# Second layer's first expert taken ahead of the overflow branch, its input by a one-hot product, and three more held weight tiles

## The chip, the cores and the metric

The kernel runs on one core of a Trainium2 chip. The metric is the device time of one execution in microseconds (us); lower is better. Weights lie in HBM and reach the core's SBUF by DMA in tiles of 512 KB. TensorE (PE) multiplies, VectorE (DVE) and ScalarE (ACT) do the elementwise work, GpSimd (POOL) issues the gathers and scatters, SyncE (SP) issues the weight loads in program order.

## What is computed

Two layers of a hybrid backbone over 256 latent and 256 context tokens of width 1024. Each layer has a token-mixing half and a mixture of 16 gated experts, of which every token uses two. The change lies in the experts of the second layer, where only the 256 latent tokens are left:

```python
def hier_moe(h, rg_w, rg_b, re_w, re_b, w_gate, w_up, w_down):
    tok = h.reshape(-1, shp[-1])
    glog = (tok @ rg_w + rg_b).astype(jnp.float32)
    gprob = jax.nn.softmax(glog, axis=-1)
    gsel = jnp.argmax(glog, axis=-1)
    ...
    top_v, top_i = lax.top_k(elog_sel, MOE_TOPK)
    top_w = jax.nn.softmax(top_v, axis=-1) * gp
    eidx = gsel[:, None] * MOE_PER_GROUP + top_i
    comb = jnp.sum(jax.nn.one_hot(eidx, N_EXPERTS, dtype=jnp.float32) * top_w[..., None], axis=1)
    out = jnp.zeros(tok.shape, jnp.float32)
    for e in range(N_EXPERTS):
        hid = jax.nn.silu(tok @ w_gate[e]) * (tok @ w_up[e])
        out = out + comb[:, e:e + 1] * (hid @ w_down[e])
```

The tokens of the change are those of `modulate(h_lat, ...)`, the normalized and modulated rows that go into `hier_moe`.

## The kernel before

**The stage.** `moe` (L1557) runs the 16 experts of a layer as places e = 0 to 15. Places 0 and 1 are the experts 0 and 1; the others are ordered by how many tokens they got, so their weights' addresses are read at run time from a table `permi`. In the second layer (`KINDS[1]`, L38) places 2, 4, 6 and 8 are heavy (up to 128 tokens, each weight split on ACT and DVE into a high and a low fp32r part, three products each) and the other twelve are light (up to 64 tokens, plain fp32 products). Each expert has 12 weight tiles of 512 KB: 4 gate, 4 up, 4 down.

**Routing, then a branch.** `route` (L1237) finds the experts of each token and the place of each token within its expert; `slots` (L1406) turns this into row indices by a product of a bf16 one-hot matrix with a small table; `light_g` (L1424) gathers the rows of an expert's tokens from a copy in HBM (`h2s`); `rank` (L1293) orders the experts and finds the largest overflow, `mxi`. Every engine reads `mxi` into a register (L1603) and jumps over a block for overflowing experts (L1604), which these inputs do not need. Only behind the branch come `by_rank` and `weights` on DVE, the transposes of the gathered rows (`light_x`, L1430) and the experts.

**The expert loop** (L1634). For each e: indices and gather of e + 2, transposes of e + 1, `hid(e)` (gate and up products, silu, product, transposes of the result), then `out(e - 1)` (down products, scaling, scatter to HBM). So the down tiles of an expert are used one expert later than its gate and up tiles: the order of use is gate and up of 0, gate and up of 1, down of 0, gate and up of 2, down of 1, and so on.

**The ring of weight tiles.** `wload2` (L1532) loads the next tile into the next place of a ring (`self.order`, L1574): 11 buffers of the rings `w` and `w2`, then tiles that are idle in this stage: 4 in `xl`, 4 in `merged`, and in the second layer 2 in `h`: 21 places. A load waits until the tile that was in its place has been used. 20 loads are issued ahead of the branch and kept in the list `hold` (L1593 to L1596): gate and up of 0 and 1, down of 0. The tile `xh` serves as four high and four low buffers for the splits (`whx`, `wlx`, L1568), beside rings of four `wh` and four `wl`. SP issues all loads in program order. All loads but those of places 0 and 1 stand behind the branch, each with its expert's number, which SP reads from `permi` (L1581).

All matmuls are recorded at L257, all transposes at L260, ACT's operations at L266 and DVE's products at L263 (helpers); tiles tell them apart.

Of the kernel before, what the change touches and what calls it, by code (L numbers as in the profile page):

```python
# [11 lines left out]
F32R = mybir.dt.float32r  # L12
# [3 lines left out]
ALU = mybir.AluOpType  # L16
AX = mybir.AxisListType
P = 128
# [170 lines left out]
class Build:  # L189
# [971 lines left out]
    def mix_out(self, l, ntt):  # L1161
        nc = self.nc
        nt = 128 * ntt
        ns = ntt // 2
        self.meta = self.sb([P, 4, 16, 9], "meta", BF16)
        stat = self.cb("meta").rearrange("p (t c) -> p t c", t=4)
        nc.gpsimd.tensor_copy(self.meta[:, :ntt], stat[:, :ntt, None, :].to_broadcast([P, ntt, 16, 9]))
        self.h = self.sb([P, 4, D], "h")
        for tt in range(ntt):
            self.load_h(l, tt, self.h[:, tt], nc.gpsimd)  # L1170
        mh = self.sb([P, KD, 512], "xh", F32R)
        ml = self.sb([P, KD, 512], "xl", F32R)
        for k in range(KD):
            self.act(mh[:, k, :nt], self.merged[:, k, :nt])
            self.tt(ml[:, k, :nt], self.merged[:, k, :nt], mh[:, k, :nt].bitcast(F32), ALU.subtract)
        s1 = self.sb([P, KD, 2], "ys1")
        s2 = self.sb([P, KD, 2], "ys2")
        m2 = self.modT[l][:, 2]
        nc.vector.tensor_scalar(s1, m2, 0.5, None, op0=ALU.mult)
        self.tt(s2, m2, self.pp("b_out")[:, :, None].to_broadcast([P, KD, 2]))  # L1180
        g1, b1 = self.row(l, "big", 0, 0), self.row(l, "big", 1, 0)
        ms = [(self.row(l, "mod", 3, s, "rowt2" if s else "rowt4"), self.row(l, "mod", 4, s, "rowt2" if s else "rowt4")) for s in range(ns)]
        yT = self.sb([P, KD, 512], "yT")

        def wout(s):
            c = slice(256 * s, 256 * s + 256)
            for dt in range(KD):
                hs = self.split(self.wload(self.a["wout"][l, dt]), pool=s == 0 and ns == 2)
                pt = self.ps()[:, :256]
                for k in range(KD):  # L1190
                    wh, wl = hs[k // 4]
                    q = slice(128 * (k % 4), 128 * (k % 4) + 128)
                    self.mm3(pt, wh[:, q], wl[:, q], mh[:, k, c], ml[:, k, c], k == 0, k == KD - 1)
                self.act(yT[:, dt, c], pt, AF.Identity, scale=s1[:, dt, s:s + 1], bias=s2[:, dt, s:s + 1])

        rw = self.rw.rearrange("p (k n) -> p k n", k=KD)
        plog = self.ps("g")
        def norms(tt):
            h1 = self.h[:, tt]
            x = self.sb([P, D], "xm")  # L1200
            for q in range(2):
                pt = self.ps()
                for k in range(4):
                    self.tr(pt[:, 128 * k:128 * k + 128], yT[:, 4 * q + k, 128 * tt:128 * tt + 128])
                c = slice(512 * q, 512 * q + 512)
                nc.vector.scalar_tensor_tensor(x[:, c], h1[:, c], ALPHA, pt, op0=ALU.mult, op1=ALU.add)
            self.norm_affine(h1, x, g1, b1, f"a{tt % 2}")
            m3, m4 = ms[tt // 2]
            self.norm_affine(x, h1, m4, m3, f"b{tt % 2}", x)
            nc.gpsimd.dma_start(self.h2s[128 * tt:128 * tt + 128, :], x)  # L1210
            return x

        def logits(tt, x):
            hT = self.sb([P, KD, P], "h2Tt")
            for q in range(2):
                pt = self.ps()
                for k in range(4):
                    self.tr(pt[:, 128 * k:128 * k + 128], x[:, 512 * q + 128 * k:512 * q + 128 * k + 128])
                self.act(hT[:, 4 * q:4 * q + 4, :].rearrange("p k t -> p (k t)"), pt)
            for k in range(KD):  # L1220
                self.mm(plog[:, 20 * tt:20 * tt + 20], hT[:, k, :], rw[:, k, :], k == 0, k == KD - 1)

        xs = {}
        for s in reversed(range(ns)):
            wout(s)
            for tt in (2 * s, 2 * s + 1):
                xs[tt] = norms(tt)
        for tt in range(2, ntt):
            logits(tt, xs[tt])
        self.pump(1)  # L1230
        logits(0, xs[0])
        logits(1, xs[1])
        self.pump(3)
        self.plog = plog
        self.dump(f"h1_{l}", self.h[:, :ntt])

    def route(self, l, ntt):  # L1237
# [48 lines left out]
        self.ix, self.m3 = self.sb([P, 16, 2], "ix", I32), self.sb([P, 16, 3], "m3")  # L1286
        stat = self.stat = self.cb("meta").rearrange("p (t c) -> p t c", t=4)
        self.slots([posm[:, :T, e] for e in range(2)], [stat] * 2, T, self.ix[:, 0:2], self.m3[:, 0:2], not KINDS[l][0])
        cnt = self.sb([P, 16], "cnt")
        v.scalar_tensor_tensor(cnt, pc[:, 64:80], 16.0, self.c("key0"), op0=ALU.mult, op1=ALU.add)  # L1290
        self.rt = gl, gmx, v1, v2, oh1, oh2, ohg, pc, cnt, posm1
# [132 lines left out]
    def light_g(self, ix, T):  # L1424
# [2 lines left out]
                                          in_offset=bass.IndirectOffsetOnAxis(ap=ix, axis=0), bounds_check=256 * T - 1, oob_is_err=False)  # L1427
        return xe

    def light_x(self, xe):  # L1430
        xT = self.sb([P, KD, P], "xTh")[:, 0:4]
        pt = self.ps("g")
        for k in range(4):
            self.tr(pt[:, 128 * k:128 * k + 128], xe[:, 128 * k:128 * k + 128])
        self.act(xT.rearrange("p k t -> p (k t)"), pt)
        return xT

    def light_hid(self, xT, wsrc):
        pgu = []
        for n in ("expert_w_gate", "expert_w_up"):  # L1440
            pt = self.ps()
# [12 lines left out]
        pt = self.ps("g")  # L1454
        for j in range(2):
            self.tr(pt[:, 128 * j:128 * j + 128], hid[:, 128 * j:128 * j + 128])
        hT = self.sb([P, 2, 512], "hidT")[:, 0, 0:256]
        self.nc.vector.tensor_copy(hT, pt[:, 0:256])
        return hT

# [69 lines left out]
                                          bounds_check=256 * T - 1, oob_is_err=False)  # L1530

    def wload2(self, src):  # L1532
        if self.hold:
            return self.hold.pop(0)
        r = self.order[self.wi % len(self.order)]
        t = self.sb([P, D], ("w", "w2")[r]) if r < 2 else self.wx[r - 2]
        self.wi += 1
        self.nc.sync.dma_start(t, src)
        return t

    def split2(self, w):
# [3 lines left out]
        for q in range(2):  # L1545
            self.si += 1
            j = self.si % self.sn
            if j < 4:
                hi, lo = self.whx[:, j], self.wlx[:, j]
            else:  # L1550
                hi, lo = self.sb([P, 512], "wh", F32R), self.sb([P, 512], "wl", F32R)
            self.act(hi, w[:, 512 * q:512 * q + 512])
            self.tt(lo, w[:, 512 * q:512 * q + 512], hi.bitcast(F32), ALU.subtract)
            hs.append((hi, lo))
        return hs

    def moe(self, l, ntt):  # L1557
        nc, tc = self.nc, self.tc
        T = ntt

        def wsrc(e, dyn):
            def f(n, u):
                if dyn:
                    return self.a[n][l, bass.ds(e, 1), u].rearrange("o p n -> (o p) n")
                return self.a[n][l, e, u]
            return f

        wx = self.sb([P, 8, 512], "xh", F32R)  # L1568
        self.whx, self.wlx = wx[:, 0:4], wx[:, 4:8]
        w3, w4 = self.sb([P, 4, D], "xl"), self.sb([P, 4, D], "merged")  # L1570
        self.wx = [w3[:, j] for j in range(4)] + [w4[:, j] for j in range(4)]
        self.wx += [self.h[:, j] for j in range(T, 4)]
        rings = (1, 0, 1, 1, 0, 1, 0, 1, 1, 0, 1) if KINDS[l][0] else (1, 0) * 5 + (1,)
        self.wi, self.order = 0, rings + tuple(range(2, 2 + len(self.wx)))  # L1574
        kind = KINDS[l]
# [11 lines left out]
        out = lambda e: (self.expert_out if kind[e] else self.light_out)(hd, wf(e), self.m3[:, e, 2:3], self.ix[:, e, 1:2], T)  # L1587
        slot = lambda e, p, m: self.slots([p[:, :T, SLOT_RANK[l][e]]], [m], T, self.ix[:, e:e + 1], self.m3[:, e:e + 1], not kind[e])
        self.route(l, T)
        g = [gather(0), gather(1)]  # L1590
        self.rank(l)
        self.pump(9)
        first = [wsrc(e, False)(n, u) for e in range(2) for n in ("expert_w_gate", "expert_w_up") for u in range(4)]  # L1593
        first += [wsrc(0, False)("expert_w_down", u) for u in range(4)]
        first = first[:len(self.order)]
        hold = [self.wload2(f) for f in first]  # L1596
        self.si = -1
        ready = [self.split2(hold[u]) for u in range(4)] if kind[0] else None
        st = self.wi, self.order
# [1 line left out]
        self.si, self.sn = -1, 4  # L1601
        tc.no_sync_barrier()
        most = nc.values_load(self.mxi[0:1, 0:1], min_val=0, max_val=576)  # L1603
        with tc.If(most > 128):  # L1604
            self.weights(T, self.by_rank(T))
            self.excess(l)
# [17 lines left out]
            self.si = -1  # L1624
            for u in range(2 if kind[0] else 0):
                self.split2(hold[u])
        self.si, self.sn = 2 * 4 - 1, 8
        self.ready = ready
        self.wi, self.order = st
        self.hold = hold  # L1630
        x, hd = getx(0), None
        oe = self.by_rank(T)
        for e in range(NE):
            if e + 2 < NE:  # L1634
# [9 lines left out]
            if e == NE - 1:  # L1644
                n = self.wi % len(self.order)
                self.wi, self.order = 0, tuple(r for r in self.order[n:] + self.order[:n] if r < 6)
            h2 = hid(e, x)
            if e:
                out(e - 1)
            if e == 0:  # L1650
# [54 lines left out]
    modT = {}  # L1705
    early = {}
    wi = si = 0
    hold = ready = None
    sn = 8

    def prologue(self, l):
# [60 lines left out]
```

## Time and profile before

| | us |
|---|---|
| median of 3 runs (lowest, highest) | 1880.85 (1872.6, 1885.78) |
| the profiled execution | 1872.98 |
| its span in the trace | 1871.2 |
| PE busy | 1716.1 (92%) |
| DVE busy | 1204.7 (64%) |
| ACT busy | 851.3 (45%) |
| POOL busy | 223.1 (12%) |

The 1.8 us between the execution's time and its span lie outside the trace. Times in rows are us from the span's start; the second layer's routing and experts take the stretch from about 1557 to 1845. A busy share is an average over many stages, so the part on the change reads one stage alone. fp32 products show as two rows per instruction.

### The profile page before, as it was taken

What the parts mean: (1) busy time and instruction counts of PE and PEld (TensorE: products, weight loads), DVE (VectorE), ACT (ScalarE), POOL (GpSimd) and SP (SyncE); (2) the same over time, 40 slices, a digit from 0 to 9 for tenths busy, and PEclk for the clock granted to TensorE, in tenths of its full rate; (3) what the DMA queues carried; (4) which work ended last, traced back from release to release, by engine and by line L of the source; (5) the groups of instructions that cost most, each with busy time, mean ns of one, the idle gap of its engine ahead of it and who ended that gap; (6) DMA issues with size and microseconds to landing.
All of it is one profiled execution on the core that took longest, in us unless ns stands there. A gap on an engine that the chain in (4) does not pass through costs nothing. (4 is left out here: it accounts for less than half of the span.)

```text
span 1871.2 us, 31716 instructions
## 1 busy us (share of the span) xinstructions
PE 1716.1 (92%) x11399; PEld 1268.0 (68%) x11399; DVE 1204.7 (64%) x2623; ACT 851.3 (45%) x1696; POOL 223.1 (12%) x321
## 2 busy tenths in 40 slices
PE   6999999998999999699999959999998995899984
PEld 1777777786777788377766516787898995566541
DVE  3878598287353547698575487698678766556203
ACT  3644553243233335187565536455555562455211
POOL 1011101000000205111111021100010100111210
PEclk9999999999999999899999979899999997899996
DMA  9221004523535745889999882231144584899993
GB/s 342 90 75 46 13 24 152 197 84 130 169 130 192 300 144 188 304 295 398 392 382 376 345 314 77 66 92 58 47 147 149 169 327 168 324 414 406 403 410 136
DMA packets 112732, 396.50 MB, mean 212 GB/s; under 512 B 16256, under 2 KB 16352, under 8 KB 112560
## 3 DMA queue, kind: packets, MB, share of 16 engines
q1 hardware_dynamic: 99120, 359.87, 52.6%
q0 software_dynamic: 13440, 34.44, 5.1%
q8 instruction: 94, 1.54, 0.3%
q14 instruction: 78, 0.64, 0.1%
HBM read 388.43 MB, written 17.35 MB: 217 GB/s over the span
## 5 line engine op out<-in xcount | busy, mean ns | idle before, releaser
L266 ACT ACTIVATE wh<-w 128x512 fp32r<-128x512 f32 x500 | 310.1, 630 | 416.8 <-PE psmm L257 293.0
L263 DVE TENSOR_TENSOR wl<-w,wh 128x512 fp32r<-128x512 f32 x484 | 333.3, 700 | 188.6 <-ACT wh L266 185.2
L257 PE MATMUL psmm<-xh,wh 128*128 128x256 f32 (+1 forms) x1280 | 440.1, 344 | 1.3 <-ACT wh L266 1.3
L257 PE MATMUL psmm<-xh,wl 128*128 128x256 f32 (+1 forms) x1280 | 434.8, 340 | 4.0 <-POOL wl L263 2.9
L257 PE MATMUL psmm<-xl,wh 128*128 128x256 f32 (+1 forms) x1280 | 433.1, 339 | 2.0 <-DVE xl L263 2.0
L257 PEld LDWEIGHTS psmm<-xh,wh 128*128 128x128 f32 x1280 | 243.1, 190 | 52.5 <-issue 16.0
L257 PEld LDWEIGHTS psmm<-xh,wl 128*128 128x128 f32 x1280 | 243.0, 190 | 38.7 <-issue 5.9
L257 PEld LDWEIGHTS psmm<-xl,wh 128*128 128x128 f32 x1280 | 243.3, 190 | 30.0 <-issue 3.9
L970 DVE SCALAR_TENSOR_TENSOR cx<-cbuf,part,cx 128x512 f32<-128x512 f32 (+1 forms) x240 | 143.0, 614 | 2.1
L257 PE MATMUL psmm<-br,wh 128*128 128x512 f32 (+1 forms) x512 | 127.9, 337 | 0.4 <-ACT cth L266 0.4
L263 DVE TENSOR_TENSOR hid<-hid,psmm 128x256 f32<-128x256 f32 (+1 forms) x32 | 17.2, 537 | 136.6 <-PE psmm L257 121.6
L257 PEld LDWEIGHTS psmm<-br,wh 128*128 128x128 f32 x512 | 87.6, 188 | 11.7 <-ACT cth L266 0.6
L263 DVE TENSOR_TENSOR xh<-w,xh 128x512 fp32r<-128x512 f32 x124 | 80.5, 686 | 18.9 <-ACT xh L266 17.9
L257 PE MATMUL psmm<-br,wl 128*128 128x512 f32 (+1 forms) x256 | 86.4, 338 | 1.1 <-DVE wl L263 1.1
L257 PE MATMUL psmm<-xh,xTh 128*128 128x512 f32 x224 | 79.4, 413 | 5.7 <-ACT xh L266 5.1
L266 ACT ACTIVATE xh<-w 128x512 fp32r<-128x512 f32 x124 | 72.2, 627 | 18.9 <-DMA w<-in_expert_w_gate_dram 7.2
L257 PE MATMUL psg<-w,silc 128*32 128x512 f32 x320 | 64.2, 651 | 16.3 <-DMA w<-in_wmod_dram 16.3
L257 PE MATMUL psmm<-w,xTh 128*64 128x256 f32 x560 | 67.6, 387 | 1.6 <-DMA w<-in_expert_w_up_dram 1.1
L266 ACT ACTIVATE ye<-psmm,m 128x512 f32<-128x512 f32 x46 | 30.3, 684 | 71.5 <-PE psmm L257 71.1
L257 PEld LDWEIGHTS psmm<-w,xTh 128*64 128x64 f32 x560 | 41.0, 139 | 26.6 <-issue 5.1
L257 PEld LDWEIGHTS psmm<-xh,xTh 128*128 128x128 f32 x224 | 40.9, 189 | 24.5 <-ACT xh L266 9.7
L266 ACT ACTIVATE xTh<-psg 128x512 fp32r<-128x512 f32 (+1 forms) x46 | 26.3, 598 | 65.4 <-PE psg L260 62.0
(471 smaller groups left out, 2847.0 us busy)
## 6 DMA issues: line engine op xcount, KB each, us to landing
w<-in_wch_dram SPq DMA_DIRECT2D x136, 512.0 KB
w<-in_wmod_dram SPq DMA_DIRECT2D x80, 512.0 KB
w<-in_expert_w_down_dram SPq DMA_DIRECT2D x77, 512.0 KB
w<-in_expert_w_gate_dram SPq DMA_DIRECT2D x76, 512.0 KB
w<-in_expert_w_up_dram SPq DMA_DIRECT2D x71, 512.0 KB
w<-in_wbr_dram SPq DMA_DIRECT2D x32, 512.0 KB
xl<-in_expert_w_up_dram SPq DMA_DIRECT2D x28, 512.0 KB
xl<-in_expert_w_gate_dram SPq DMA_DIRECT2D x26, 512.0 KB
```

What stands on the lines that cost most here:

```text
L257: self.nc.tensor.matmul(out, lhsT, rhs, start=start, stop=stop, **k)
L263: (eng or self.nc.vector).tensor_tensor(out, a, b, op)
L266: self.nc.scalar.activation(out, in_, func, **k)
L970: nc.vector.scalar_tensor_tensor(x, w, dw[:, c, k:k + 1], x, op0=ALU.mult, op1=ALU.add)
```

## The change

For a layer whose place 0 is light (the second one) the rows of expert 0 are no longer gathered from HBM. `light_x0` builds an fp32 one-hot matrix from the places found by `route` and multiplies it with the two token tiles that are still on chip (`self.h2t`), which gives the transposed input at once. `hid(0)` is emitted between the reading of `mxi` and the branch. The list `hold` becomes a table `held`, and loads are keyed by expert, name and tile. Three parts of `xh` join the ring of weight tiles (24 places), the fourth holds the input and the hidden rows of expert 0, and the splits of the second layer use the rings `wh` and `wl` alone. As many loads as the ring has places are issued ahead of the branch: the down tiles of expert 1 come to those of before.

```diff
+        self.h2t = xs
...
+        self.posm0 = posm[:, :T, 0]
...
+    def light_x0(self, T, xT):
+        oh = self.sb([P, 4, P], "oh")[:, :T, 0:64]
+        for tt in range(T):
+            self.nc.vector.tensor_scalar(oh[:, tt], self.cb("iota")[:, 0:64], self.posm0[:, tt:tt + 1], None, op0=ALU.is_equal)
+        pt = self.ps("g")
+        for k in range(KD):
+            o = 128 * (k % 4) + 64 * (k // 4)
+            for tt in range(T):
+                self.mm(pt[:, o:o + 64], self.h2t[tt][:, 128 * k:128 * k + 128], oh[:, tt], tt == 0, tt == T - 1, skip_group_check=True)
+        self.act(xT.rearrange("p k t -> p (k t)"), pt)
+        return xT
...
-        if self.hold:
-            return self.hold.pop(0)
+        if isinstance(src, tuple):
+            return src[0]
...
-            if j < 4:
+            if j < 4 and self.whx is not None:
...
-                return self.a[n][l, e, u]
+                return held.pop((e, n, u), self.a[n][l, e, u])
...
-        wx = self.sb([P, 8, 512], "xh", F32R)
-        self.whx, self.wlx = wx[:, 0:4], wx[:, 4:8]
+        if KINDS[l][0]:
+            wx = self.sb([P, 8, 512], "xh", F32R)
+            self.whx, self.wlx = wx[:, 0:4], wx[:, 4:8]
...
+        if not KINDS[l][0]:
+            self.whx = None
+            w5 = self.sb([P, 4, D], "xh")
+            self.wx += [w5[:, j] for j in range(3)]
...
-        g = [gather(0), gather(1)]
+        g = [gather(0), gather(1)] if kind[0] else [gather(1)]
+        x0 = None if kind[0] else self.light_x0(T, w5[:, 3, 0:512].rearrange("p (k t) -> p k t", k=4))
...
-        first = [wsrc(e, False)(n, u) for e in range(2) for n in ("expert_w_gate", "expert_w_up") for u in range(4)]
-        first += [wsrc(0, False)("expert_w_down", u) for u in range(4)]
-        first = first[:len(self.order)]
+        keys = [(e, n, u) for e in range(2) for n in ("expert_w_gate", "expert_w_up") for u in range(4)]
+        keys += [(e, "expert_w_down", u) for e in range(2) for u in range(4)]
+        keys = keys[:len(self.order)]
+        first = [wsrc(e, False)(n, u) for e, n, u in keys]
         hold = [self.wload2(f) for f in first]
+        held.update((k, (t,)) for k, t in zip(keys, hold))
...
         most = nc.values_load(self.mxi[0:1, 0:1], min_val=0, max_val=576)
+        h0 = None if kind[0] else self.light_hid(x0, wf(0), w5[:, 3, 512:768])
         with tc.If(most > 128):
...
-        x, hd = getx(0), None
+        x, hd = getx(0) if x0 is None else x0, None
...
-            h2 = hid(e, x)
+            h2 = h0 if e == 0 and h0 is not None else hid(e, x)
```

The order of instructions shows three places. First PE, second layer, from the jump over the overflow block on, in the kernel before (`xe_17765` and `xe_17769` are the gathered rows of experts 0 and 1, `oh_18569` the one-hot matrix for the indices of place 2, `w_...` weight tiles):

```order
L1604 UNCONDITIONAL_BRANCH x2
L260 MATMUL psg_18549<-ident_77,xe_17765 128x128 x4
L257 LDWEIGHTS oh_18569
L257 MATMUL psg_18568<-constb_79,oh_18569 128x9
L260 MATMUL psg_18581<-ident_77,xe_17769 128x128
L257 LDWEIGHTS oh_18569
L257 MATMUL psg_18568<-constb_79,oh_18569 128x9
L260 MATMUL psg_18581<-ident_77,xe_17769 128x128 x3
L257 MATMUL psmm_18587<-w_3365_17794,xTh_18548 64x256 x4
```

The transposes of expert 0, the indices of place 2 and the transposes of expert 1 stand ahead of the products of expert 0.

PE in the changed kernel, same stage, ahead of the branch (`xm_...` are the token tiles, `oh_17769` the new fp32 one-hot matrix, `xh_17702` the part that holds the input of expert 0):

```order
L257 MATMUL psg_17772<-oh_17769,xm_17590 128x64
L257 MATMUL psg_17772<-oh_17769,xm_17624 128x64
L257 MATMUL psmm_17861<-w_3366_17811,xh_17702 64x256 x4
L257 MATMUL psmm_17861<-w_17813,xh_17702 64x256 x4
L257 MATMUL psmm_17861<-w_3368_17815,xh_17702 64x256 x4
L257 MATMUL psmm_17861<-w_17817,xh_17702 64x256 x4
L257 MATMUL psmm_17878<-w_3370_17819,xh_17702 64x256 x4
L257 MATMUL psmm_17878<-w_17821,xh_17702 64x256 x4
L257 MATMUL psmm_17878<-w_3372_17823,xh_17702 64x256 x4
L257 MATMUL psmm_17878<-w_17825,xh_17702 64x256 x4
L260 MATMUL psg_17898<-ident_77,hid_17895 128x128 x2
L1626 TENSOR_LOAD mxi_17803
```

The pair of one-hot products stands there eight times; all of `hid(0)` on PE lies ahead of PE's reading of `mxi`, and on DVE and ACT their parts of it do too. Behind the branch PE now begins so:

```order
L1628 UNCONDITIONAL_BRANCH x2
L257 LDWEIGHTS oh_18768
L257 MATMUL psg_18767<-constb_79,oh_18768 128x9
L260 MATMUL psg_18780<-ident_77,xe_17765 128x128 x2
L257 LDWEIGHTS oh_18768
L257 MATMUL psg_18767<-constb_79,oh_18768 128x9
L260 MATMUL psg_18780<-ident_77,xe_17765 128x128 x2
L257 MATMUL psmm_18862<-w_3374_17827,xTh_18779 64x256 x4
```

The first thing there is the product for the indices of place 2, whose matrix DVE makes behind its own branch; the transposes of expert 1 (`xe_17765` here) and its gate products follow it.

On SP all 14 readings of `permi`, each with two register instructions, now stand between the reading of `mxi` and the branch; before, they stood behind it. The third place is SP behind the branch, at the 22nd to 25th load there in the kernel before (places 2 and 4; an ISA row sets the address register of a load):

```order
L1538 DMA h_17267<-in_expert_w_down_dram 128x1024
L1538 ISA
L1538 DMA w_3539_19048<-in_expert_w_down_dram 128x1024
L1538 ISA
L1538 DMA w_19064<-in_expert_w_down_dram 128x1024
L1538 ISA
L1538 DMA w_3556_19116<-in_expert_w_gate_dram 128x1024
```

The gate tiles of place 4 go into ring buffers `w` there, which had held gate and up tiles of place 2. In the changed kernel the same loads are the 19th to 22nd behind the branch:

```order
L1552 DMA merged_17701<-in_expert_w_down_dram 128x1024
L1552 ISA
L1552 DMA h_17267<-in_expert_w_down_dram 128x1024
L1552 ISA
L1552 DMA h_17267<-in_expert_w_gate_dram 128x1024
L1552 ISA
L1552 DMA xh_17702<-in_expert_w_gate_dram 128x1024
```

The four gate tiles of place 4 now go into the second part of `h` and the three parts of `xh`, where the down tiles of expert 1 are held.

## Rows read from the trace of the kernel before

**Rows 1.** Stretches of the stage: busy us of each engine (instructions), PE's granted clock, DMA share, GB/s

```profile
1550.00:1600.00 50.00, 24.43 (x153) 21.59 (x153) 32.00 (x104) 11.31 (x21) 4.40 (x5) 0.64 0.40 145
1600.00:1650.00 50.00, 49.03 (x321) 30.53 (x318) 27.69 (x71) 22.27 (x40) 5.55 (x5) 0.99 1.00 392
...
1750.00:1800.00 50.00, 47.62 (x354) 26.16 (x354) 6.28 (x17) 7.41 (x14) 7.20 (x7) 1.00 1.03 408
```

**Rows 2.** The chain that ended last, its part before the end: start, us, what

```profile
1812.20 9.90 DMA xl<-in_expert_w_up_dram
...
1822.22 10.18 DMA w<-in_expert_w_down_dram
...
1832.54 13.72 PE psmm L257 x26
```

**Rows 3.** Timeline of SP: start, us from first to last, what it issues

```profile
1595.31 0.35 SPq L1538 DMA_DIRECT2D h<-in_expert_w_gate_dram  x1
1600.25 2.56 SPq L1538 DMA_DIRECT2D w<-in_expert_w_gate_dram  x3
1603.35 2.92 SPq L1538 DMA_DIRECT2D w<-in_expert_w_up_dram  x4
1606.80 3.45 SPq L1538 DMA_DIRECT2D w<-in_expert_w_down_dram  x4
...
1626.68 4.68 SPq L1538 DMA_DIRECT2D w<-in_expert_w_gate_dram  x4
```

**Rows 4.** Timeline of PE: start, us, operation, count [idle before <-releaser]

```profile
1577.27 3.60 PE L257 MATMUL psg<-rw,h2Tt 128*128 128x20 f32 x16
1586.31 0.68 PE L257 MATMUL psg<-constb,oh 128*128 128x9 bf16 x4 [0.78 <-DVE oh L1416]
1594.68 1.09 PE L260 MATMUL psg<-ident,xe 128*128 128x128 f32 x4 [7.69 <-DVEq L1604]
...
1598.23 9.81 PE L257 MATMUL psmm<-w,xTh 128*64 128x256 f32 x74
1608.87 0.44 PE L260 MATMUL psg<-ident,hid 128*128 128x128 f32 x2 [0.82 <-DVE hid L263]
...
1633.36 1.07 PE L257 MATMUL psmm<-w,hidT 128*64 128x512 f32 x2
...
1647.60 2.35 PE L257 MATMUL psmm<-xh,hidT 128*128 128x512 f32 x9
...
1797.21 0.44 PE L260 MATMUL psg<-ident,hid 128*128 128x128 f32 x2 [0.59 <-DVE hid L263]
```

**Rows 5.** Timeline of DVE around the branch, and a copy of hidden rows

```profile
1586.00 0.74 DVE L1416 TENSOR_SCALAR oh<-constb,posm 128x128 bf16<-128x128 bf16 x4
...
1594.55 0.29 DVE L1327 TENSOR_TENSOR oe<-ohg,oh 128x32 f32<-128x32 f32 x2 [4.59 <-DVEq L1604]
...
1609.93 0.42 DVE L1458 COPY hidT<-psg 128x256 f32<-128x256 f32 x1
```

**Rows 6.** Timeline of ACT: the input of expert 1, copied from PSUM

```profile
1598.39 0.60 ACT L266 ACTIVATE xTh<-psg 128x512 f32<-128x512 f32 x1 [1.84 <-issue]
```

**Rows 7.** Lines L1604 and L1581 on SP: ns min/median/max, first and last start

```profile
L1604 SPq EVENT_SEMAPHORE  x9: 17/17/17, 1593.6 to 1594.2; - x9
L1604 SPq COMPARE_BRANCH  x1: 53/53/53, 1590.7 to 1590.7; - x1
L1581 SPq FUSED_REGOPS  x4: 147/147/147, 1596.0 to 1597.7; - x4
```

**Rows 8.** Short stretches, columns as in rows 1

```profile
1570.00:1580.00 10.00, 9.88 (x45) 9.35 (x46) 5.20 (x7) 2.68 (x5) 1.08 (x2) 0.50 0.26 105
...
1600.00:1602.00 2.00, 2.00 (x16) 1.27 (x14) 2.00 (x10) 1.36 (x2) 0.00 (x0) 0.73 0.76 223
```

**Rows 9.** The lone load's stretch: us, granted clock, DMA share, GB/s

```profile
1598.00:1599.00 1.00, 0.50 0.36 131
```

**Rows 10.** Low parts of split weights, 1598 to 1834: busy us, mean ns | idle before

```profile
L263 DVE TENSOR_TENSOR wl<-w,wh 128x512 fp32r<-128x512 f32 x38 | 24.5, 687 | 1.9 <-ACT wh L266 1.9
```

More of the change, by code (lines that the diff above doesn't have):

```diff
@@ L1436, in light_x, with light_hid @@
         return xT
-    def light_hid(self, xT, wsrc):
+    def light_hid(self, xT, wsrc, hT=None):
         pgu = []
@@ L1456, in light_hid @@
             self.tr(pt[:, 128 * j:128 * j + 128], hid[:, 128 * j:128 * j + 128])
-        hT = self.sb([P, 2, 512], "hidT")[:, 0, 0:256]
+        hT = self.sb([P, 2, 512], "hidT")[:, 0, 0:256] if hT is None else hT
         self.nc.vector.tensor_copy(hT, pt[:, 0:256])
@@ L1559, in moe @@
         T = ntt
+        held = {}
         def wsrc(e, dyn):
@@ L1626, in moe @@
                 self.split2(hold[u])
+        hold = None
         self.si, self.sn = 2 * 4 - 1, 8
@@ L1629, in moe @@
         self.wi, self.order = st
-        self.hold = hold
-        x, hd = getx(0), None
+        x, hd = getx(0) if x0 is None else x0, None
         oe = self.by_rank(T)
@@ L1707 @@
     wi = si = 0
-    hold = ready = None
+    ready = None
     sn = 8
```

## The prediction, made before the changed kernel ran

> **What bounds the kernel now.** I read the stretches first [rows 1], then the chain that ended last [rows 2], then the timelines of the queues that meet there [rows 3 to 7]. In the 50 us around the second layer's routing PE is busy 24.43 us and DMA has a share of 0.40; from 1600 on DMA stands at 1.00 or more, at 392 to 408 GB/s, and PE at 47 to 49 of 50 us [rows 1]. So the expert stage has two limits that lie close together. The chain settles which ends last: hops of some 10 us from one weight load's issue to another's, then 13.72 us of PE [rows 2]. A load of 0.524 MB takes 1.28 us at 408 GB/s, so a hop is a queue of eight loads. Hence the end is the time at which the stream of loads is let go, plus the loads left. Whatever delays one load in an unbroken stream delays the end by as much; whatever PE gains matters only through the places it frees.
>
> In the kernel before the stream starts at 1595.31 with one load and goes on from 1600.25, as fast as PE frees places [rows 3]: the place of expert 0's last up tile is free at 1606.80. By 1626.68 the loads come in fours over 4.7 us, 1.3 us each, which is DMA's own pace: the 45th load of the stage, the first gate tile of place 4, is queued behind eight others and lands one hop later, some 10.2 us, at 1636.9 [rows 2, 3].
>
> **The change, part by part.** *Expert 0's input.* The one-hot products can start when the index products end, 1586.31 + 0.68 = 1586.99 [rows 4], and DVE has made two more small matrices behind the four that end at 1586.74 [rows 5]; I take 1587.15. They are 16 fp32 instructions, 32 rows with a 128x128 weight load each. The nearest rows are the router's logits, 16 in 3.60 us, 0.225 each [rows 4]: 7.2 us. The bound below is half of that, 3.6 us, if the full clock is granted; above, the gathered rows' transposes, 4 in 1.09 us, 0.27 each: 8.7. I take 7.2, since the logit rows have the same form (many weight loads, few columns) and ran at a granted clock of 0.50, as everything around them did. Copy 0.60 [rows 6] and two semaphores: expert 0's gate starts at 1595.1, where before it starts at 1598.23 [rows 4]. So the gather, two transposes and a wait for the branch are traded for 3.1 us. Its gate and up take what they took, 1598.23 to 1606.78, 8.55 us with the first 3 us at half clock: they end at 1603.65.
>
> [...]
>
> *The branch.* Before, PE ran from expert 0 straight into expert 1. Now all of `hid(0)` stands ahead of the jump on PE and DVE, and expert 1 behind it. After the last up product: DVE's product and PE's transposes, 0.59 + 0.44 [rows 4], the copy 0.42 [rows 5] with a semaphore, 1.5 us: 1605.15. Then DVE's wait from its last operation to the first behind the branch, 4.59 us [rows 5]: 1609.75. Behind it PE's first instruction is the index product of place 2, so PE waits for DVE's `by_rank` too; from DVE's first operation there to the end of expert 1's input copy on ACT it took 1594.55 to 1598.39 + 0.60, 4.44 us [rows 5, 6]. Expert 1's gate starts at 1614.25, where before it started at 1606.78: 7.5 us later.
>
> [...] The idle 0.82 us and the transposes of `hid(0)`, 0.44 [rows 4], no longer lie between expert 1 and what follows: -1.3. So PE reaches `out(1)`, before at 1633.36 [rows 4], 7.8 us later, at 1641.2.
>
> [...] The trace has SP's compare at 1590.7 and its next instruction at 1593.6 [rows 7], so the jump itself costs 2.9 us here. [...]
>
> *The ring.* SP now reads 14 numbers ahead of its branch, at (1597.7 - 1596.0) / 3 = 0.57 us each [rows 7]: 8 us. From 1590.7 that gives its branch at about 1599 and the first load at 1603, against 1600.25. This costs little: eight loads into expert 0's places, eight when expert 1 frees its own from 1615.7 on, four more as `out(0)` does. Those 20 loads are 25.6 us of DMA, done by about 1632. The next four, place 4's gate, stand in the places of expert 1's down tiles, and these are used only by `out(1)`. Before, the same loads waited for nothing but DMA. Now the 45th is let go when the first down tile of `out(1)` is done, 1641.2 + 1.0 = 1642.2, and, with nothing ahead of it, lands about 3.3 us later (the lone load of 1595.31 left DMA a share of 0.36 from 1598 to 1599 [rows 9], so it ended by about 1598.6): 1645.5 against 1636.9, **8.6 us later**, after a hole of some 10 us in the stream. SP issues in order, so all loads wait with it. The three added places and four earlier loads buy nothing, since both kernels have issued 44 loads at that point and 148 remain. From there DMA runs as before, and so does the tail: 11 + 4 places in both.
>
> *The splits.* Four buffer pairs instead of eight. A pair costs DVE 0.687 us [rows 10]; PE takes nine such products in 2.35 us [rows 4], about 0.75 for the three of a pair. So DVE keeps up, but four pairs let it run ahead by some 3 us only. Cover: at the end PE goes at DMA's pace, 8 x 1.28 = 10.2 us for the gate and up of a light expert against 6.9 when they lie ready; over the last two experts that is 6.6 us of slack, 1.6 per heavy expert. I take 0; without that cover, every us lost goes to the end.
>
> *The rest.* The gather of expert 0 (POOL, hidden), four loads more in a stretch in which DMA has a share of 0.40 [rows 1], the first layer: 0. A small gain is possible where 24 places bridge a late release, some 0.5 us; I take it off. Sum: 8.6 - 0.5 = +8.1 us on the profiled execution, 1872.98 to 1881.1. That execution was near the lowest of the runs shown; on their median the same sum gives 1880.85 + 8.1 = 1889.0. A measurement of this kernel can tell about 1% from no change, 19 us, so this counts as no change.
>
> **The rivals.** [...]
>
> *The lead survives.* If `out(1)` came early enough for the stream to stay whole, the three loads of lead count: 3 x 1.3 = 3.9 us, less 2.8 for SP's later start, and up to 3 us that DMA then starts earlier: -1 to -5, on the median about 1877.5. It needs PE at expert 1 by about 1607, so a jump and a `by_rank` that together cost nothing.
>
> *The splits throttle (slower).* If four pairs do not cover the other work of ACT and DVE between the splits (two output copies of 0.7, two input copies of 0.6, silu, hidden rows: an estimate of 4 us per heavy stretch against 3 of cover), each of the eight stretches (gate and up, then down, of four experts) loses 1.5 to 3.5 us, 12 to 28. Beyond PE's 6.6 us of slack this adds 5 to 21 to the 8.1: on the median about 1902. It counts as slower, by over 19 us, from 2.2 us a stretch on. For it: DVE's 0.687 is close to PE's 0.75. Against it: before, DVE waited 1.9 us in all for ACT on these splits [rows 10], so the engines that split are not short of time.
>
> **How the numbers follow.** Forecast 0.62, clock 0.17, lead 0.09, splits 0.12. Bounds of the forecast's own terms (one-hot 3.6 to 8.7, climb 0 to 3.2) give +3 to +11. The range goes from the lead's -5, with 2 us for a median that scatters, to the lower half of the splits: 1874 to 1900. Faster by over 1% needs more than any case holds, left at 0.03 for what I missed; slower takes most of the splits and a little of the forecast, 0.10; same 0.87.
>
> **What would show it.** PE's first gate product of expert 1 some 10 us after expert 0's last, and behind DVE; a hole in DMA's share at about 1632 to 1643; the first load into the second part of `h` released by PE's `out(1)`; the end shifted by as much. Wrong if DMA shows no hole, if the clock is 1.0 before 1595, or if heavy experts show PE waits of over 2 us for ACT or DVE.

## The result, and the profile of the changed kernel

The changed kernel took 1.0079 of the time of the kernel before (95% interval 1.0054 to 1.0105; medians 1893.29 and 1877.94 us): slower by some 15 us, within the 1% that the forecast had called no change. Its profiled execution took 1886.93 us, with a span of 1885.2. It holds four tiles more ahead of the branch than before, 24 against 20, in three places more; the title's "three more held weight tiles" are the places.

Whole executions scatter by 10 to 20 us. Where one kernel was profiled twice (runs 10 and 12, and the changed kernel with run 11), its layers ahead of the change took up to 13 us more or less and the stage of the change less than 1, so the experiments also go by one stage: from PE's first index product of the second layer's routing (1585.23 in the kernel before, 1587.04 in the changed one) to the end of the span. It took 286.0 us before and 298.2 after, 12.2 more. The two traces stand 1.81 us apart at its start, which is taken off below where times of both are compared.

PE's timeline, in the columns of [rows 4]:

```profile
1588.12 0.68 PE L257 MATMUL psg<-constb,oh 128*128 128x9 bf16 x4 [0.78 <-DVE oh L1418]
1588.77 7.09 PE L257 MATMUL psg<-oh,xm 128*128 128x64 f32 x32
1596.55 3.68 PE L257 MATMUL psmm<-w,xh 128*64 128x256 f32 x16 [0.69 <-ACT xh L266]
...
1607.24 0.44 PE L260 MATMUL psg<-ident,hid 128*128 128x128 f32 x2 [0.60 <-DVE hid L263]
1617.42 0.19 PE L257 MATMUL psg<-constb,oh 128*128 128x9 bf16 x1 [9.74 <-DVE oh L1418]
...
1619.45 2.82 PE L257 MATMUL psmm<-w,xTh 128*64 128x256 f32 x10 [0.74 <-ACT xTh L266]
...
1646.63 1.07 PE L257 MATMUL psmm<-h,hidT 128*64 128x512 f32 x2
1647.63 0.66 PE L260 MATMUL psg<-ident,hid 128*128 128x128 f32 x4
1648.22 0.64 PE L257 MATMUL psmm<-h,hidT 128*64 128x512 f32 x1
...
1648.70 0.59 PE L257 MATMUL psmm<-h,hidT 128*64 128x512 f32 x1
```

The one-hot products (7.09 us) bring expert 0 forward: its gate starts at 1596.55, or 1594.74 on the clock of the trace before, against 1598.23 [rows 4]. Then comes what the kernel before did not have: PE stands for 9.74 us between expert 0 and expert 1, and what ends that is DVE's one-hot matrix for place 2. `out(1)` starts at 1646.63; before, at 1633.36.

SP's timeline, as [rows 3]:

```profile
1604.46 2.11 SPq L1552 DMA_DIRECT2D w<-in_expert_w_gate_dram  x4
1606.81 2.30 SPq L1552 DMA_DIRECT2D w<-in_expert_w_up_dram  x4
1621.46 3.87 SPq L1552 DMA_DIRECT2D w<-in_expert_w_gate_dram  x3
...
1635.09 0.33 SPq L1552 DMA_DIRECT2D h<-in_expert_w_down_dram  x1
1649.32 0.33 SPq L1552 DMA_DIRECT2D h<-in_expert_w_gate_dram  x1
```

The last row is the 45th load of the stage. SP stands in front of it for 14 us, until PE is done with the first down tile of `out(1)`: two products, four rows, of which the last starts at 1648.70. Stretches, in the columns of [rows 1], show the hole that follows in DMA, and the clock:

```profile
1600.00:1602.00 2.00, 2.00 (x12) 1.18 (x10) 0.00 (x0) 0.00 (x0) 0.00 (x0) 0.50 0.00 0
1602.00:1604.00 2.00, 2.00 (x18) 1.21 (x16) 0.00 (x0) 0.39 (x1) 0.00 (x0) 0.85 0.01 4
...
1600.00:1650.00 50.00, 38.77 (x226) 23.01 (x224) 23.76 (x85) 17.95 (x32) 5.55 (x4) 0.84 0.63 231
...
1643.00:1650.00 7.00, 7.00 (x33) 3.95 (x33) 3.91 (x7) 3.02 (x7) 0.00 (x0) 1.00 0.06 19
...
1750.00:1800.00 50.00, 47.24 (x343) 26.39 (x338) 9.62 (x24) 10.32 (x20) 8.55 (x9) 1.00 1.03 404
```

Where [rows 1] have a DMA share of 1.00 for 1600 to 1650, it is now 0.63, and 0.06 from 1643 to 1650, around the issue of the 45th load. From 1650 to 1800 both kernels have 1.01 or more. The clock stays at 0.50 from 1587 to 1602, through all of the one-hot products and most of expert 0's gate and up; from 1602 to 1604 it is 0.85.

DVE's timeline around the branch:

```profile
1607.72 0.42 DVE L1472 COPY xh<-psg 128x256 f32<-128x256 f32 x1 [0.53 <-PE psg L260]
1614.85 0.29 DVE L1329 TENSOR_TENSOR oe<-ohg,oh 128x32 f32<-128x32 f32 x2 [6.71 <-DVEq L1628]
```

The branch's own line by engine, in the columns of [rows 7]:

```profile
L1628 DVEq EVENT_SEMAPHORE  x2: 21/21/21, 1614.6 to 1614.7; - x2
L1628 DVEq COMPARE_BRANCH  x1: 63/63/63, 1609.3 to 1609.3; - x1
...
L1628 PEldq COMPARE_BRANCH  x1: 5965/5965/5965, 1609.0 to 1609.0; - x1
...
L1628 SPq EVENT_SEMAPHORE  x9: 17/17/17, 1603.6 to 1604.2; - x9
L1628 SPq COMPARE_BRANCH  x1: 53/53/53, 1601.1 to 1601.1; - x1
```

The time from the compare to the next instruction of the same engine is the jump: 2.5 us on SP, 5.3 on DVE. Before, DVE's jump ended in a wait of 4.59 us [rows 5]; this one makes it 6.71. On PE the compare's own row lasts as long as the jump: 6.0 us, to 1615.0. So PE itself was back 2.4 us before its first product at 1617.42; `by_rank` on DVE fills those. The chain's end, as [rows 2]:

```profile
1838.92 10.20 DMA w<-in_expert_w_down_dram
1849.26 10.59 PE psmm L257 x28
```

The stream of loads still sets the end: 10 us hops, then PE's last products. The last hop starts 14.9 us later than before (16.7 less the 1.81), but the products behind it take 10.59 us where they took 13.72 [rows 2].

### The profile page after: what moved, and what is told of

It reads as the page before. It is cut to its first block, busy times and chain, and to the rows that moved or that the text cites. A ratio compares the mean times of both kernels' runs of the same rounds, so it can differ in the third digit from the quotient of the medians.

```text
span 1885.2 us, 31793 instructions
## 1 busy us (share of the span) xinstructions
PE 1722.8 (91%) x11427; PEld 1273.1 (68%) x11427; DVE 1205.3 (64%) x2625; ACT 854.0 (45%) x1697; POOL 224.6 (12%) x320
## 5 line engine op out<-in xcount | busy, mean ns | idle before, releaser
L257 PEld LDWEIGHTS psmm<-xl,wh 128*128 128x128 f32 x1280 | 243.0, 190 | 30.4 <-issue 3.9
L257 PE MATMUL psg<-w,silc 128*32 128x512 f32 x320 | 64.4, 652 | 16.5 <-DMA w<-in_wmod_dram 16.5
L257 PE MATMUL psmm<-xh,xTh 128*128 128x512 f32 (+1 forms) x232 | 66.2, 405 | 3.8 <-ACT xh L266 2.7
L257 PE MATMUL psmm<-w,xTh 128*64 128x256 f32 x488 | 61.9, 390 | 3.2 <-DMA w<-in_expert_w_up_dram 1.1
L263 DVE TENSOR_TENSOR xh<-w,xh 128x512 fp32r<-128x512 f32 x86 | 55.9, 685 | 9.6 <-ACT xh L266 7.9
L257 PE MATMUL psmm<-wh,xTh 128*128 128x512 f32 x144 | 57.3, 398 | 0.7 <-ACT wh L266 0.7
L257 PE MATMUL psmm<-wl,xTh 128*128 128x512 f32 x144 | 57.0, 396 | 0.3 <-DVE wl L263 0.3
L266 ACT ACTIVATE xh<-w 128x512 fp32r<-128x512 f32 x86 | 50.3, 627 | 13.3 <-DMA w<-in_expert_w_gate_dram 6.1
L257 PE MATMUL psmm<-wh,xTl 128*128 128x512 f32 x144 | 56.3, 391 | 0.0
```

Of the source, the lines that this page charges most:

```text
L257: self.nc.tensor.matmul(out, lhsT, rhs, start=start, stop=stop, **k)
L263: (eng or self.nc.vector).tensor_tensor(out, a, b, op)
L266: self.nc.scalar.activation(out, in_, func, **k)
```

## The experiments

Theory G is that of the prediction: the end follows the time at which the 45th load is let go. Rivals: P, the time that PE loses at the branch sets the end; S, four split pairs cost the time; and C for the jump: it takes longer while weight loads fill DMA. Times "in the stage" are from the first index product to the end of each profiled span; "last load" is the issue of the last weight load, from the same start. Between the two lies the tail: 44.5 to 44.9 us in the kernel before and in runs 3 and 5, 42.0 to 42.2 in all others (last section). So a difference of 2.7 us in the stage can be the tail's alone, and what the stream of loads gained or lost is read from the last load.

| kernel | ratio to before (95%) | last load, us | stage, us |
|---|---|---|---|
| before | 1 | 241.1 | 286.0 |
| changed | 1.0079 (1.0054 to 1.0105) | 256.0 | 298.2 |
| 1: 20 held | 1.0048 (1.0024 to 1.0071) | 247.9 | 289.9 |
| 2: expert 0 behind the branch | 1.0025 (0.9997 to 1.0054) | 244.7 | 286.7 |
| 3: old places and splits | 1.0038 (1.0007 to 1.0069) | 250.9 | 295.4 |
| 4: first load late | 1.0061 (1.0034 to 1.0087) | 253.6 | 295.7 |
| 5: before, four pairs | 0.9992 (0.9974 to 1.0010) | 240.5 | 285.4 |
| 6: `by_rank` ahead | 1.0055 (1.0022 to 1.0088) | 256.2 | 298.4 |
| 7: 1 and 2 together | 0.9996 (0.9978 to 1.0014) | 239.6 | 281.7 |
| 8: 7, place 2's gate held | 0.9998 (0.9981 to 1.0016) | 243.1 | 285.1 |
| 9: one-hot input alone | 1.0015 (0.9993 to 1.0037) | 243.0 | 285.2 |
| 10: before, 25 places | 0.9977 (0.9954 to 1.0000) | 238.6 | 280.7 |
| 11: changed, again | one execution | 256.7 | 298.9 |
| 12: 10 again | 0.9976 (0.9955 to 0.9997) | 238.0 | 280.2 |

**1. Only 20 tiles held.**

```diff
-keys = keys[:len(self.order)]
+keys = keys[:len(self.order) if kind[0] else 20]
```

> The changed kernel, but of the 24 places only 20 are filled ahead of the branch: expert 1's four down tiles are loaded behind it, in the order of use. Theory G (the end follows the let-go of the 45th load, which in the changed kernel waits for out(1)): four loads start at once behind SP's branch (about 1604), the 45th waits only for place 2's first gate tile; DMA shows no hole between 1643 and 1650, the 45th load lands at 1638 to 1642, and the kernel takes 1.000 to 1.004 of the kernel before, though PE still reaches expert 1 some 12 us late. Theory P (PE's own lost time sets the end): 1.007 to 1.010, as the changed kernel. Theory S (four split pairs cost the time): 1.007 to 1.010 too, with PE waits for ACT or DVE in the heavy experts.

The stretch in which the changed kernel has its hole, as [rows 1], first in this run, then in the changed kernel:

```profile
1640.00:1655.00 15.00, 15.00 (x72) 9.45 (x72) 8.66 (x18) 7.76 (x15) 0.97 (x1) 1.00 1.03 412
1640.00:1655.00 15.00, 15.00 (x80) 9.21 (x80) 10.56 (x20) 8.63 (x16) 1.82 (x2) 1.00 0.49 184
```

Share 1.03; the changed kernel has 0.49 in the same 15 us. The stage is 8.3 us shorter, though PE is as late at expert 1 as in the changed kernel (its up products are done 43.5 us behind the first index product in both). So P falls as the whole account, and the held tiles, with the hole they make, cost 8.3 us. The ratio came out a little above G's range, and its interval reaches P's; the stage decides. The last load still goes out 6.8 us later than in the kernel before, of which the shorter tail leaves 3.9 in the stage.

**2. Expert 0's gate and up behind the branch.**

```diff
-h0 = None if kind[0] else self.light_hid(x0, wf(0), w5[:, 3, 512:768])
...
-h2 = h0 if e == 0 and h0 is not None else hid(e, x)
+h2 = self.light_hid(x, wf(0), w5[:, 3, 512:768]) if e == 0 and x0 is not None else hid(e, x)
```

> The changed kernel, with the one-hot input ahead of the branch but expert 0's gate and up behind it, so that PE goes from expert 0 straight to expert 1; 24 places and 24 held as in the changed kernel. Theory G: out(1) comes at about 1632 and lets the 45th load go at 1635 instead of 1649, after a hole of some 9 us that began earlier; it lands at about 1638, and the kernel takes 1.000 to 1.003 of the kernel before. Theory P: the same, 1.000 to 1.003, as PE loses no time at the branch. Theory S: 1.007 to 1.010, since the four pairs stay.

1.0025 and 286.7 us: as G and P expected, while S falls, since the four pairs are all still there. A hole remains ahead of the 45th load, at 1633.70, and the last load goes out 3.6 us later than in the kernel before; the tail, 2.9 us shorter, hides most of that. The stretch from 1629 to 1634, as [rows 1]:

```profile
1629.00:1634.00 5.00, 5.00 (x24) 2.51 (x24) 4.42 (x7) 2.95 (x5) 0.00 (x0) 1.00 0.16 61
```

**3. The old places and splits, with the input and expert 0 ahead of the branch.** 20 tiles are held as in run 1, and expert 0's input and hidden rows stand in buffers of their own.

```diff
-if KINDS[l][0]:
-    wx = self.sb([P, 8, 512], "xh", F32R)
-    self.whx, self.wlx = wx[:, 0:4], wx[:, 4:8]
+wx = self.sb([P, 8, 512], "xh", F32R)
+self.whx, self.wlx = wx[:, 0:4], wx[:, 4:8]
...
-    w5 = self.sb([P, 4, D], "xh")
-    self.wx += [w5[:, j] for j in range(3)]
```

> The changed kernel with the weight places and split buffers of the kernel before (21 places, 20 held, eight split pairs); the one-hot input and expert 0's gate and up ahead of the branch stay. Theory G: the 45th load waits for the fourth gate tile of place 2, at about 1640 with PE as late as in the changed kernel, and lands at about 1646, some 7 us after that of the kernel before: 1.003 to 1.005. Theory P: 1.007 to 1.010. Theory S: 1.000 to 1.002, since the eight pairs are back.

1.0038, in G's range. In the stage it costs 9.4 us, more than G's 7, and S, which expected nothing here, falls: the branch alone, without the held down tiles, is dear too where only 21 places bridge it.

**4. The first load held back.** Run for C: were the weight loads in DMA what made DVE's jump long?

```diff
+for _ in range(0 if kind[0] else 36):
+    nc.values_load(self.permi[0:1, 0:1], engines=[mybir.EngineType.SP], min_val=0, max_val=NE - 1)
 h0 = None if kind[0] else self.light_hid(x0, wf(0), w5[:, 3, 512:768])
```

> The changed kernel with 36 more reads of one number on SP, which hold the first load behind the branch back from 1604.4 to about 1617. [...]

The branch's line on DVE:

```profile
L1630 DVEq EVENT_SEMAPHORE  x2: 21/21/21, 1621.4 to 1621.6; - x2
L1630 DVEq COMPARE_BRANCH  x1: 63/63/63, 1618.4 to 1618.4; - x1
```

The stretch of that jump, in the columns of [rows 1], then that of DVE's jump in the changed kernel and in the kernel before:

```profile
1618.00:1621.50 3.50, 0.00 (x0) 0.00 (x0) 0.00 (x0) 0.00 (x0) 0.00 (x0) 0.83 0.03 7
...
1609.00:1615.00 6.00, 0.00 (x0) 0.00 (x0) 0.15 (x2) 0.00 (x0) 0.00 (x0) 0.54 1.01 396
...
1591.00:1594.50 3.50, 0.00 (x0) 0.00 (x0) 0.00 (x0) 1.00 (x1) 0.10 (x1) 0.50 0.17 42
```

The jump is back at 3.0 us, with DMA at 0.03; in the changed kernel it took 5.3 with DMA at 1.01. The first load came 13.5 us later behind the first index product, and the stage still was 2.5 us shorter. This bears C out: with the loads out of its way the jump is 2.3 us shorter, where a jump long by its place or length would have stayed at 5.3. And an early first load was worth nothing there. What in the jump waits is not shown.

**5. The kernel before with four split pairs.**

```diff
+self.whx = None
+if KINDS[l][0]:
+    wx = self.sb([P, 8, 512], "xh", F32R)
+    self.whx, self.wlx = wx[:, 0:4], wx[:, 4:8]
...
-            if j < 4:
+            if j < 4 and self.whx is not None:
```

> The kernel before, with nothing changed but the split buffers of the second layer: four pairs in place of eight. Theory G (the end follows the let-go of the loads): 0.998 to 1.002 of the kernel before, and no more than 1 us of PE waits for ACT or DVE per heavy expert. Theory S (four pairs cost time): 1.004 or more.

The low parts of the split weights, as [rows 10]:

```profile
L263 DVE TENSOR_TENSOR wl<-w,wh 128x512 fp32r<-128x512 f32 x76 | 48.4, 687 | 10.7 <-ACT wh L266 10.5
```

In the kernel before, the 38 splits of [rows 10] are only half of these; the others use the buffers in `xh`:

```profile
L263 DVE TENSOR_TENSOR xh<-w,xh 128x512 fp32r<-128x512 f32 x38 | 24.7, 687 | 9.3 <-ACT xh L266 9.2
```

0.9992, and 285.4 us. DVE waits 10.5 us for ACT on these 76 splits, against 1.9 + 9.2 = 11.1 before: four pairs make it wait no longer. PE waits 2.3 us for ACT's splits in both kernels. So S falls by itself.

**6. `by_rank` ahead of the branch**, beside expert 0.

```diff
+oe = None if kind[0] else self.by_rank(T)
 h0 = None if kind[0] else self.light_hid(x0, wf(0), w5[:, 3, 512:768])
...
-oe = self.by_rank(T)
+oe = self.by_rank(T) if kind[0] else oe
```

> The changed kernel, with DVE's by_rank ahead of the branch (in the time in which PE makes expert 0's input, gate and up), so that behind the branch DVE begins with the one-hot of place 2. Theory G: expert 1's gate comes 1.8 to 2.5 us earlier behind expert 0, out(1) and the let-go of the 45th load as well, and the kernel takes 1.005 to 1.008 of the kernel before, 1.5 to 2.5 us less than the changed one from the routing to the end. Rival (PE's own jump, which shows no row of its own, would end the wait anyway): nothing gained, 1.007 to 1.010.

PE's first row behind the branch:

```profile
1620.34 0.19 PE L257 MATMUL psg<-constb,oh 128*128 128x9 bf16 x1 [8.41 <-DVE oh L1418]
```

PE's own jump:

```profile
L1629 PEldq COMPARE_BRANCH  x1: 6705/6705/6705, 1613.2 to 1613.2; - x1
```

A miss for G: the wait fell by 1.3 us only (9.74 to 8.41), the 45th load came 0.7 us earlier, and the stage did not get shorter. The rival said why, though PE's jump does have a row: it took 6.7 us here, to 1619.9, and PE's first product follows 0.4 us later. DVE's matrix, which the row names, was itself held up for 0.2 us by PE's side of the branch. So with `by_rank` out of the way, PE's jump ends the wait. The ratio's interval holds both answers.

**7. Both edits, of runs 1 and 2.**

> Both edits of the two earlier runs in one: expert 0's gate and up behind the branch, and 20 of 24 places filled ahead of it. Theory G: four loads start at once behind SP's branch (about 1596 to 1598), no hole follows, the 45th load lands some 4 to 5 us earlier than in the kernel before, and the kernel takes 0.996 to 1.000 of it. If the two edits only added up (8.3 us from the held tiles, 11.5 from the branch, by the time from the routing to the end), it would be 7 to 8 us faster than the kernel before: 0.995 to 0.997. Rival (the four places more and the earlier start buy nothing, as DMA is full anyway): 1.000 to 1.003.

281.7 us in the stage, 4.3 less than before, but the last load goes out only 1.5 us earlier, the rest being the tail's, and the ratio is 0.9996: its interval holds a small gain and none. The two edits don't add up (8.3 and 11.5 alone, 16.5 together). The branch's place still makes 8.2 us between runs 1 and 7, where there is no such hole: the first load leaves 17.4 us behind the first index product in run 1 and 10.4 in run 7. SP's 14 reads stand ahead of its branch in the one and behind it in the other, which fits; PE's lateness at expert 1 differs too.

**8. Place 2's gate tiles held.** They are the next in order of use, in place of the four left free in run 7. Expert 0's gate and up stay behind the branch, and `wsrc` is adapted (not shown) so that SP reads place 2's expert ahead of it.

```diff
-keys = keys[:len(self.order)]
+keys = keys[:len(self.order)] if kind[0] else keys[:20] + [(2, "expert_w_gate", u) for u in range(4)]
```

> As the run before it, but the four added places are filled ahead of the branch with place 2's gate tiles, the next in order of use (SP reads that place's expert ahead of the branch). Theory G: these four loads start at about 1592, in a stretch in which DMA stands nearly idle, 4 to 6 us earlier than behind the branch; the stream's end comes earlier by up to that: 0.993 to 0.998 of the kernel before, and 2 to 5 us less than the run before it from the routing to the end. Rival (the stream is held up later by PE, so that an earlier start is given back): the same as the run before it.

The branch's line on DVE and SP:

```profile
L1627 DVEq EVENT_SEMAPHORE  x2: 21/21/21, 1607.7 to 1607.8; - x2
L1627 DVEq COMPARE_BRANCH  x1: 63/63/63, 1603.4 to 1603.4; - x1
...
L1627 SPq EVENT_SEMAPHORE  x9: 17/17/17, 1610.4 to 1611.8; - x9
L1627 SPq COMPARE_BRANCH  x1: 53/53/53, 1605.2 to 1605.2; - x1
```

The stretch of these jumps, as [rows 1]:

```profile
1605.00:1610.00 5.00, 0.62 (x3) 0.43 (x3) 0.29 (x2) 0.60 (x1) 0.00 (x0) 0.50 0.97 383
```

Neither theory: the stage is 3.4 us longer than in run 7. The four loads, let go at 1602.8 to 1604.4, fill DMA (0.97) just as the engines jump: DVE takes 4.3 us, SP 5.3. So the lead is paid back at the branch, in the way that run 4 shows.

**9. The one-hot input alone**, on the places, splits and branch of the kernel before.

```diff
-g = [gather(0), gather(1)]
+g = [gather(0), gather(1)] if kind[0] else [gather(1)]
+x0 = None if kind[0] else self.light_x0(T, self.sb([P, 520], "cbuf")[:, 0:512].rearrange("p (k t) -> p k t", k=4))
```

> The kernel before with the first part of the change alone: expert 0's input by the one-hot product, its gate and up behind the branch, 21 places, 20 held, eight split pairs. Theory G: the branch ends at about the time of the input's copy, so expert 0 starts within 1 us of the kernel before and nothing follows from it: 0.998 to 1.002 of the kernel before, 285 to 287 us from the routing's first index product to the end (286.0 before). Rival (the one-hot product is itself what makes the changed kernel late): 1.003 or more.

PE's timeline:

```profile
1594.76 7.09 PE L257 MATMUL psg<-oh,xm 128*128 128x64 f32 x32
1605.86 4.53 PE L257 MATMUL psmm<-w,cbuf 128*64 128x256 f32 x18 [4.01 <-ACTq L1622]
```

As G expected, 1.0015 and 285.2; the last load goes out 1.9 us later, and the tail is 2.7 shorter. The product is done early, but ACT copies it ahead of its own jump, and PE waits 4.01 us for that: expert 0 starts 12.8 us behind the first index product, against 13.0 with the gather. Alone, this part gains nothing here.

**10 and 12. The kernel before with 25 places.**

```diff
 self.wx += [self.h[:, j] for j in range(T, 4)]
+if not KINDS[l][0]:
+    w5 = self.sb([P, 4, D], "xh")
+    self.wx += [w5[:, j] for j in range(4)]
```

It has run 5's edit as well, since the room of the other four pairs is used.

> The kernel before with nothing of the change but more places: 25 instead of 21 (four split pairs, since their room is taken), 20 of them filled ahead of the branch as before, the gather and expert 0 as before. Theory G: five loads in place of one start behind SP's branch, the stream is whole from then on and ends some 5 us earlier: 280 to 283 us from the routing's first index product to the end against 286.0, and 0.996 to 0.999 of the kernel before. Rival (an earlier start is given back, as DMA is full anyway): 0.9995 to 1.002.

> The kernel of the run with 25 places once more, unchanged, for a second interval. If the 5.3 us gained from the routing to the end are the kernel's own, the time there is within 1 us of 280.7 again and the ratio 0.995 to 0.999; if the first interval's 0.9977 was scatter of the layers before it, the ratio comes out at 0.9995 to 1.002 while the time from the routing to the end stays.

SP's timeline behind the branch, in run 10:

```profile
1608.29 0.35 SPq L1538 DMA_DIRECT2D h<-in_expert_w_gate_dram  x1
1608.85 2.43 SPq L1538 DMA_DIRECT2D xh<-in_expert_w_gate_dram  x3
1611.47 0.33 SPq L1538 DMA_DIRECT2D xh<-in_expert_w_up_dram  x1
```

Five loads go out behind the branch where one did [rows 3]. 280.7 and 280.2 us in the stage; 0.9977 and 0.9976. The second interval lies below 1, the first ends at it, so by these runs it is some 0.2% faster than the kernel before. Of the 5.3 us in run 10, 2.5 are the stream's (the last load is issued 238.6 us behind the first index product, against 241.1), half of what G expected; the rest is the shorter tail, below.

**11. The changed kernel again.**

> The changed kernel once more, unchanged, for a second profile. If the time from the routing's first index product to the end is a property of the kernel and not of one execution, it is within 1 us of 298.2, with the jump of DVE at 5 to 6 us, while the start of the routing scatters by several us between executions.

298.9 us, with DVE's jump at 5.8: the stage repeats within 1 us. Its start moved by 1.3 us here, and by 13 between runs 10 and 12, which are one kernel.

## Why the prediction was right, and where its terms were off

The direction, the size as no change within 1%, and the mechanism held: an end some 8 us later was forecast, through a later `out(1)`, a hole in DMA ahead of the 45th load, and a stream that ends later by as much. Run 1 shows the hole as its larger part: 8.1 of the 14.9 us by which the last load is late. The size was short, 8.1 against 12.2 us in the stage, and that it missed by no more is luck: the terms that missed nearly all point to slower, and a tail that nobody forecast took 2.7 us off.

- *Expert 0's input.* 7.2 us forecast, 7.09 measured; the gate at 1595.1, measured 1594.74. Half clock was the right choice: as in [rows 8], PE was busy (7.74 of 8 us from 1588 to 1596) and was granted 0.50, up to 1602. A full clock there, which had the chance of 0.17, was not granted.
- *Gate and up of expert 0.* Taken as 8.55 us, since they "take what they took"; measured 1596.55 to 1606.65, 10.1. This term was too small because the clock rose some 3 us behind the gate's start before (0.73 from 1600 to 1602 [rows 8]), and some 6 now (0.85 from 1602 to 1604). With the earlier start that makes 1.2 us.
- *DVE's wait at the branch.* 4.59 forecast, 6.71 measured: 2.1 us. The row of before was from an idle DMA (0.17 from 1591 to 1594.5); behind expert 0 the jump meets the eight loads that expert 0's places have let go (1.01 from 1609 to 1615). Run 4 shows it, run 8 again.
- *by_rank to expert 1's gate.* 4.50 with its semaphore forecast, 4.60 measured: 0.1 us. Expert 1's gate to `out(1)`: 26.95 forecast, 27.18 measured: 0.2 us. The forecast's 7.8 us up to `out(1)` are 7.5 less 1.3, and 1.6 for a climb of the clock within expert 1; that term was an estimate, and no run shows it by itself: in the changed kernel the clock was 0.50 up to 1623, some 3.5 us behind the start of expert 1's gate, and 0.96 from 1623 to 1624.
- *The let-go of the 45th load.* 1.0 us behind `out(1)`'s start forecast, 2.7 measured: the tile is read by two products (four rows), and the transposes of place 2's hidden rows and products of other tiles lie between them. 1.7 us.
- *SP's reads.* "This costs little" was true beside the hole (run 4). Without a hole it may not be: between runs 1 and 7 the first load is 7.0 us apart, and the stage 8.2. No run moves the reads alone, so their share isn't shown.
- *The stream behind the hole.* 8.6 and these 1.2, 2.1, 0.1, 0.2 and 1.7 make 13.9; the last load was issued 14.9 us later (1843.0 less 1.81, against 1826.3). The gain of 0.5 us from 24 places isn't seen, and 1 us stays open. DMA's hole came later than forecast and was some 7 us long, not 10.
- *The tail*, forecast as the same, is 2.7 us shorter by the clock (0.53 from 1836 to 1846 before, 1.00 from 1850 to 1857 now). 14.9 less 2.7 is the 12.2. No run shows that the change is what made it shorter.
- *The splits.* 0 forecast; runs 2 and 5 bear it out, and in the changed kernel PE waits for a split once, 0.7 us. But the reading that DVE waited "1.9 us in all" took half of the splits for the whole: the other half waited 9.2 (run 5), so the argument against that rival was weaker than it looked. The 6.9 us in the forecast's cover are twice the 3.45 from 1603.35 to 1606.80 [rows 3].

On the median the forecast was 1889.0, measured 1893.29. The ratio's interval, 10 to 20 us, holds the stage's 12.2; that anything ahead of the routing belongs to the change isn't shown.

## What to carry to other kernels

Fill places ahead of time only in the order of use: in a ring whose loads go out in order, one tile that is held early and used late stops every load behind it (here for 14 us; without it, in run 1, the stage was 8.3 us shorter). An early start in the right order can still be given back, as run 8 shows (3.4 us more than run 7). Work put ahead of a branch puts the branch behind that work, on every engine that takes part, and the loads which that work lets go can then meet the jump (DVE's took 5.3 us with DMA at 1.01, and 3.0 at 0.03 in run 4). Where whole executions scatter more than the effect, time a stage from one of its own instructions to the end, and look at the clock in its tail before a gain is believed (44.9 us of tail before, 42.2 in the changed kernel).

## What the runs showed of the hardware that was not expected

*The jump took longer with weight loads in DMA.* From compare to next instruction it took 2.4 to 3.0 us with little in DMA, a share of 0.28 or less (SP, ACT and DVE in the kernel before and in run 4), and 4.3 to 6.0 with weight loads in DMA, a share of 0.68 to 1.03 (DVE in the changed kernel and in runs 1, 3, 6, 8 and 11, ACT and SP in run 8). On PE it took 3.5 in the kernel before and 3.8 in run 4, against 6.0 to 6.8 in the changed kernel and in runs 1, 3 and 6. What in the jump waits is not shown.

*The clock of the last products.* In both kernels PE runs its last products, behind the last down tile, without a break, yet in the kernel before the clock fell to 0.50 some 11 us ahead of their end, in the changed one some 1 us ahead. First the kernel before, in a stretch not shown above:

```profile
1836.00:1846.00 10.00, 10.00 (x16) 2.58 (x15) 0.00 (x0) 2.48 (x4) 0.98 (x1) 0.53 0.01 1
```

The clock falls at 1836.6 there, 4 us into these products. And the changed kernel:

```profile
1850.00:1857.00 7.00, 7.00 (x22) 1.78 (x21) 0.00 (x0) 2.18 (x4) 0.98 (x1) 1.00 0.09 33
```

From the last load's issue to the end it was 44.9 us before, 44.5 and 44.9 in runs 3 and 5, and 42.0 to 42.2 in the changed kernel and all other runs. The three slow ones have 21 places, but so has run 9, with 42.2. The cause stays open; no run was made for it, and whether the tail belongs to the kernel or to the execution isn't shown.
